# First layer of a hybrid decoder step: in 8 of 24 units a chunk's second part moves directly ahead of the next chunk's first part

## The chip, the cores and the metric

The kernel runs on one core of one Trainium2 chip. The metric is the device time of one launch in microseconds; the time before is the median of three runs. Profiles come from one separate, profiled execution.

## The reference

One inference step of a two-layer decoder with model width 1024, for a prompt of 512 positions and 8 samples of 4 positions, which share the weights. The first layer is a Mamba-2 (SSD) mixer with 32 heads of 64 in 4 groups, state size 128; the second is a dilated sliding-window attention. The heart of the first layer, where the change lies, is the chunked scan (T = 128, four chunks for the prompt):

```python
a_cs = jnp.cumsum(A, axis=-1)
seg = jnp.exp(jnp.where(tri, a_cs[..., :, None] - a_cs[..., None, :], -jnp.inf))
cb = jnp.einsum("bctgn,bcsgn->bcgts", Cc, Bc)
m = jnp.einsum("bcgts,bgjcts->bcgjts", cb, seg)
y_diag = jnp.einsum("bcgjts,bcsgjp->bctgjp", m, X)
chunk_states = jnp.einsum("bctgn,bgjct,bctgjp->cbgjpn", Bc, decay_in, X)
...
y_off = jnp.einsum("bctgn,cbgjpn,bgjct->bctgjp", Cc, s_in, jnp.exp(a_cs))
```

In words: each chunk builds a decaying causal mask m, gives an output within the chunk from m, hands a state to the next chunk, and adds what the incoming state contributes. Ahead of it stand a norm, the input projection and a convolution of width 4 with SiLU; behind it a gate with z, a norm and the output projection. The samples do the same for their 4 positions from a given state.

## The kernel before

All large products (projections, attention) run on TensorE (PE) with weights split into a high and a low part: a weight tile is loaded by the SP queue (wraw, L196), copied to whi by ScalarE (ACT, L205), and the rest goes to wlo on VectorE (DVE, L206). One projection tile is 48 matmuls, 24 into the PSUM tile pa and 24 into pb. In the first layer these matmuls are *filler*: a generator (filler_a, L882) yields after each of them, and run(n) (L899) takes n.

Between stretches of filler stand 24 *units*, for each of 4 groups of heads: chunk 0, chunk 1, quad 0, chunk 2, chunk 3, quad 1. A chunk (ssm_chunk, L720) is 128 prompt positions; a quad (ssm_quad, L782) is four samples.

A chunk has two parts, divided by a yield.

- First part: the mask tile m is loaded by the SP queue (L728; a row of cumulated decays, spread over all partitions, 512 KB) and turned into a decay on ACT (L730 eight times, L732). TensorE makes cbp (a transpose and a product) and xp (four transposes of xs). ACT copies btok, DVE makes xdt, xdd (L746, L747), cbm (L748) and multiplies m by it (L749). For chunks 1 to 3 the tile ea is loaded (L754).
- Second part: TensorE makes csp from xdd and btok, yo from the old state (chunks 1 to 3) and yd from m and xdt. POOL (GpSimd) and DVE form the new state st (L761, L762; chunk 0: a copy on ACT, L769), DVE makes ea from yo (L767) and v from yd and ea (L778; chunk 0: a copy on ACT, L776).

A quad has three parts: loads of sample states s (L804) and small products; yds, yot and three updates up, each added to s on DVE (L862) and written back (L863, ACT's queue); and a fourth update.

Buffers: m has two, xdt and xdd share three, ea has one, s five, wraw three, whi and wlo two each. In PSUM the tag ss (all tiles of units) has five buffers and the tag pj (pa, pb) three.

The loop at L915 places the parts. For unit u: first part of u, pace // 2 filler matmuls, second part of u-1, the rest of the pace, third part of u-1. The pace per unit is 57, 62, 64 or 44, by group. A chunk's third call finds its generator at its end. skip_one (L698) puts a skip product (L703) and the gate (L711) on DVE and POOL; its four calls per unit stay where they are.

The order of each engine's instructions is fixed ahead of the run by the framework's scheduler: it follows program order as priority, and takes an instruction when, by its own estimate of times, the inputs and a buffer are ready. Matmuls and transposes are held in program order from L430 on (pin, L139). Each engine, and the SP queue, then works down its list and waits where an input or buffer is late.

The tiles named in the steps are: wraw, whi, wlo (weights), cb, co, xs (convolution, L343 to L645), m, cbm, xdt, xdd, csp, yo, yd, st, ea, v (chunks), s, up (quads).

Of the kernel before, what the change touches and what calls it, by code (L numbers as in the profile page):

```python
# [127 lines left out]
def tile_yoco_step(  # L128
# [569 lines left out]
    def skip_one():  # L698
        if not skips:
            return  # L700
        g, i = skips.pop(0)
        vi = v_t[g][:, i, :]
        nc.vector.scalar_tensor_tensor(vi, xs_t[g][:, i, :], dsk[:, 4 * g + i:4 * g + i + 1], vi, op0=ALU.mult, op1=ALU.add)  # L703
        v_done.add((g, i))
        if i < z_done.get(g, 0):
            gate_mul_a(g, i)
# [192 lines left out]
    def run(n):  # L899
        for _ in range(n):  # L900
            if next(fill, 0) == 0:
                return

    units = [(f, (g, i)) for g in range(4) for f, i in
             ((ssm_chunk, 0), (ssm_chunk, 1), (ssm_quad, 0), (ssm_chunk, 2), (ssm_chunk, 3), (ssm_quad, 1))]
# [8 lines left out]
    live = []  # L914
    for u in range(len(units) + 1):  # L915
        pace = PACE[min(u, len(units) - 1) // 6]
        if u < len(units):
            live.append(units[u][0](*units[u][1]))
            next(live[u])
        skip_one()  # L920
        run(pace // 2)
        if u:
            next(live[u - 1], 0)
            skip_one()
            run(pace - pace // 2)
            next(live[u - 1], 0)
            if u == len(units):
                run(10000)
            if u % 6 == 0:
                skips += [(u // 6 - 1, i) for i in range(4)]  # L930
            skip_one()
        else:
            run(pace - pace // 2)
# [702 lines left out]
    def run(n):  # L1636
        m = min(n, ahead[0]) if n > OCN else 0
        ahead[0] -= m
        for _ in range(n - m):
            if next(fill, 0) == 0:  # L1640
                return

    units = [(f, (h, i)) for h in range(ATH - 1) for f, i in
             ((attend, 0), (sample, 0), (attend, 1), (attend, 2), (sample, 1), (attend, 3))]
# [6 lines left out]
    live = []  # L1651
# [113 lines left out]
```

## Time and profile before

| | us |
|---|---|
| median of three runs | 927.66 |
| lowest and highest | 925.65, 928.69 |
| profiled execution, its own time | 932.11 |
| its span | 930.2 |

The profile's span is the stretch from the first to the last recorded instruction; 1.9 us of the execution lie around it. Rows of a timeline give the start in us from the span's start, the duration, the engine, the line, the operation, and what was written and read; a bracket at the end gives the idle time just before it and what ended it. Several like instructions in a row are merged ("x3"). Rows of waits give who waited, on which line, for whom: total us, times, longest. Rows of windows give, for a stretch, its length and the busy time (and count) of PE, PEld, DVE, ACT and POOL, then the granted TensorE clock, the busy share of the DMA engines and GB/s. PEld is TensorE's loading of weights, which overlaps its matmuls.

### The profile page before, as it was taken

The page shows a single profiled execution, that of the slowest core. Times are in us where ns is not written, and L with a number is a line of the kernel's source. Part 1 is how long each engine was busy: PE and PEld are TensorE (multiplying, and loading weights), DVE is VectorE, ACT ScalarE, POOL GpSimd, SP SyncE. Part 2 cuts the span into 40 slices and gives each one's busy share as a digit, 9 for nine tenths or more (in the row PEclk, how much of TensorE's full clock was granted, in tenths as well). Part 3 has the DMA queues.
Part 4 walks back from the last instruction along what each step waited for, and adds up shares of the span by engine and source line. Part 5 has one row for each costly group of instructions (what it writes and reads, how often), then busy time and mean ns, then how long its engine had stood idle before and what let it go on. Part 6 is the DMA issues. An engine that isn't in the chain of part 4 may idle for free.

```text
span 930.2 us, 21888 instructions
## 1 busy us (share of the span) xinstructions
PE 908.9 (98%) x8671; PEld 847.9 (91%) x8671; DVE 687.5 (74%) x1435; ACT 489.9 (53%) x1140; POOL 163.0 (18%) x212
## 2 busy tenths in 40 slices
PE   8999999999999999999999999999999999999997
PEld 7989888888989889999999999999899999989997
DVE  6998899989799899644489335876677766778732
ACT  6678655655566655422255213555455555557642
POOL 2031344433514642111101001000000000000021
PEclk9999999999999999999999999999999999999999
DMA  8224365355364442536277556757768868774511
GB/s 295 93 74 155 104 206 166 121 170 170 134 201 161 149 165 101 156 108 228 90 256 227 183 184 196 265 182 264 252 203 262 280 204 267 270 256 155 194 49 49
DMA packets 80573, 168.48 MB, mean 181 GB/s; under 512 B 19990, under 2 KB 37736, under 8 KB 79960
## 3 DMA queue, kind: packets, MB, share of 16 engines
q1 hardware_dynamic: 73784, 154.60, 50.5%
q10 hardware_dynamic: 5616, 9.75, 2.8%
q0 software_dynamic: 1072, 2.74, 1.1%
q8 instruction: 68, 1.11, 0.5%
q14 instruction: 33, 0.27, 0.1%
HBM read 141.14 MB, written 25.93 MB: 180 GB/s over the span
## 4 chain that ended last, share of the span: by engine, by line
PE 82%; DVE 9%; DMA 4%; ACT 2%; issue 2%; POOL 0%; SPq 0%; POOLq 0%; DVEq 0%; ACTq 0%
PE pa L146 33%; PE pb L146 28%; PE sp L146 3%; PE pv L146 2%; PE so L146 2%; PE s L146 2%; DVE wlo L206 2%; DMA kc<-ck 1%; PE yd L146 1%; DMA m<-aed 1%; DVE co L641 1%; PE csp L146 1%; PE w L149 1%; PE ptp L149 1%; PE xp L149 1%
## 5 line engine op out<-in xcount | busy, mean ns | idle before, releaser
L205 ACT ACTIVATE whi<-wraw 128x1024 fp32r<-128x1024 f32 x69 | 72.8, 1056 | 97.0 <-PE pb L146 57.2
L206 DVE TENSOR_TENSOR wlo<-wraw,whi 128x1024 fp32r<-128x1024 f32 x69 | 89.6, 1298 | 45.1 <-ACT whi L205 44.7
L146 PE MATMUL pa<-bq,whi 128*128 128x272 f32 x512 | 103.1, 296 | 0.0
L146 PE MATMUL pb<-nl,whi 128*128 128x288 f32 x280 | 84.0, 300 | 0.0
L146 PE MATMUL pb<-nh,wlo 128*128 128x288 f32 x280 | 83.5, 298 | 0.0
L146 PE MATMUL pb<-nh,whi 128*128 128x288 f32 x280 | 83.4, 298 | 0.0
L146 PEld LDWEIGHTS pa<-bq,whi 128*128 128x128 f32 x512 | 81.2, 189 | 0.9
L146 PE MATMUL pa<-nh,whi 128*128 128x256 f32 x280 | 81.1, 290 | 0.5 <-DVE uz L681 0.5
L146 PE MATMUL pa<-nl,whi 128*128 128x256 f32 x280 | 80.7, 288 | 0.0
L146 PE MATMUL pa<-nh,wlo 128*128 128x256 f32 x280 | 80.1, 286 | 0.0
L146 PE MATMUL pb<-bq,whi 128*128 128x272 f32 x384 | 77.2, 296 | 1.3 <-DVE kv L1230 1.1
L146 PE MATMUL pa<-bq,wlo 128*128 128x272 f32 x256 | 74.2, 290 | 0.0
L641 DVE SCALAR_TENSOR_TENSOR co<-cb,cvp,co 128x568 f32<-128x568 f32 x72 | 64.0, 892 | 1.5 <-ACT co L639 0.9
L146 PEld LDWEIGHTS pb<-bq,whi 128*128 128x128 f32 x384 | 60.8, 189 | 2.6 <-DVE kv L1230 1.3
L1289 ACT ACTIVATE whi<-wraw 128x512 fp32r<-128x512 f32 x64 | 40.1, 627 | 35.2 <-PE pb L146 16.8
L146 PEld LDWEIGHTS pb<-nl,whi 128*128 128x128 f32 x280 | 53.0, 189 | 4.4 <-issue 4.4
L146 PEld LDWEIGHTS pa<-nh,whi 128*128 128x128 f32 x280 | 53.8, 192 | 2.6 <-issue 1.9
L146 PE MATMUL pb<-bq,wlo 128*128 128x272 f32 x192 | 55.5, 289 | 0.0
L146 PEld LDWEIGHTS pa<-nl,whi 128*128 128x128 f32 x280 | 53.8, 192 | 1.4 <-issue 1.4
L146 PEld LDWEIGHTS pb<-nh,wlo 128*128 128x128 f32 x280 | 53.1, 190 | 2.2 <-issue 2.2
L146 PEld LDWEIGHTS pa<-nh,wlo 128*128 128x128 f32 x280 | 53.8, 192 | 0.9 <-issue 0.9
L146 PEld LDWEIGHTS pb<-nh,whi 128*128 128x128 f32 x280 | 53.0, 189 | 0.8 <-issue 0.8
(408 smaller groups left out, 2788.0 us busy)
## 6 DMA issues: line engine op xcount, KB each, us to landing
wraw<-w_in SPq DMA_DIRECT2D x40, 512.0 KB
kc<-ck SPq DMA_DIRECT2D x32, 640.0 KB
vc<-cv SPq DMA_DIRECT2D x32, 640.0 KB
wraw<-wb SPq DMA_DIRECT2D x32, 512.0 KB
s<-s SPq DMA_DIRECT2D x32, 256.0 KB
m<-aed SPq DMA_DIRECT2D x16, 512.0 KB
ssmS<-s ACTq DMA_DIRECT2D x32, 256.0 KB
wraw<-w_out SPq DMA_DIRECT2D x16, 512.0 KB
```

What stands on the lines that cost most here:

```text
L146: pin(nc.tensor.matmul(*a, **k))
L149: pin(nc.tensor.transpose(*a))
L205: a = nc.scalar.activation(hi, raw, AF.Copy)
L206: b = lo_eng.tensor_tensor(lo, raw, f32(hi), op=ALU.subtract)
L641: nc.vector.scalar_tensor_tensor(o, cb[:, k:k + n], cvp[:, ti, k:k + 1], o, op0=ALU.mult, op1=ALU.add)
L1289: nc.scalar.activation(hi, src[p][j], AF.Copy)
```

## The change

Where unit u-1 and unit u are both chunks (chunks 0 and 1, chunks 2 and 3 of each group: 8 units), the second part of u-1 is called directly ahead of the first part of u, and no longer between the two stretches of filler behind it. Everything else, the filler's amounts included, stays.

```diff
     for u in range(len(units) + 1):
         pace = PACE[min(u, len(units) - 1) // 6]
+
+        joined = 0 < u < len(units) and units[u - 1][0] is units[u][0] is ssm_chunk
+        if joined:
+            next(live[u - 1], 0)
         if u < len(units):
             live.append(units[u][0](*units[u][1]))
             next(live[u])
         skip_one()
         run(pace // 2)
         if u:
-            next(live[u - 1], 0)
+            if not joined:
+                next(live[u - 1], 0)
             skip_one()
             run(pace - pace // 2)
-            next(live[u - 1], 0)
+            if not joined:
+                next(live[u - 1], 0)
             if u == len(units):
                 run(10000)
```

## The prediction

> **What bounds the kernel now.** I read the page's engine rows first, then the list of waits for the first layer, then the timeline around each wait of TensorE. The page says that TensorE sets the time.
>
> ```profile
> span 930.2 us, 21888 instructions
> PE 908.9 (98%) x8671; PEld 847.9 (91%) x8671; DVE 687.5 (74%) x1435; ACT 489.9 (53%) x1140; POOL 163.0 (18%) x212
> ```
>
> TensorE is busy for 908.9 of 930.2 us. The change neither adds nor removes a matmul, so it can win or lose only through TensorE's waits, its clock, and the switches between kinds of matmul. In the first layer's stretch of the trace the list of waits has these of TensorE, in total, count and longest:
>
> ```profile
> PE xp L149 <- DVE xs L644: 2.1, 1, 2.1
> PE up L146 <- DVE cbm L748: 1.4, 1, 1.4
> PE yd L146 <- ACT yos L825: 1.2, 1, 1.2
> ```
>
> They cost more than they show. Around the first two, the table by windows (busy time of the engines, then the granted clock) reads:
>
> ```profile
> 187.00:198.00 11.00, 11.00 (x92) 10.23 (x92) 11.00 (x18) 5.97 (x19) 0.40 (x1) 1.00 0.71 232
> 215.60:219.10 3.50, 3.50 (x18) 3.50 (x18) 3.50 (x6) 3.09 (x9) 0.00 (x0) 0.51 0.37 90
> 260.00:263.40 3.40, 3.40 (x17) 3.40 (x16) 3.38 (x8) 2.03 (x4) 0.00 (x0) 0.51 0.27 106
> ```
>
> Behind the wait of 2.1 us the granted clock is 0.51 for 3.50 us, which loses 3.50 x 0.49 = 1.7 us; behind the wait of 1.4 us it is 0.51 for 3.40 us, again 1.7 us. So the first costs 2.1 + 1.7 = 3.8 us (call it stall B, at 214 us), the second 1.4 + 1.7 = 3.1 us (stall C, at 258 us). The third cost its 1.2 us alone.
>
> The Trainium skill ("TensorE: Matmul & The Clock Gate", Part 1: The HAM clock gate) states that the clock halves after at least one idle window of about 3.4 us. The trace agrees on the halving and on how long it lasts (0.51 for 3.4 and 3.5 us), but not on the trigger: waits of 2.1 and 1.4 us were enough. By the page's trigger stall B would be worth its wait alone, and with the 0.4 us for switches below the forecast would be 927.66 - 0.4 - 2.1 = 925.2.
>
> Where do the stalls come from? For stall B, the timelines of the SP queue, ACT, DVE and TensorE, in order of time:
>
> ```profile
> 189.12 6.29 SPq L804 DMA_DIRECT2D s<-s  x3
> 195.46 0.42 SPq L196 DMA_DIRECT2D wraw<-w_in  x1
> 195.97 0.38 SPq L728 DMA_DIRECT2D m<-aed  x1
> ...
> 203.81 0.99 ACT L730 ACTIVATE m<-m,tok 128x128 f32<-128x128 f32 x3 [3.10 <-DMA m<-aed]
> 206.34 1.05 ACT L205 ACTIVATE whi<-wraw 128x1024 fp32r<-128x1024 f32 x1
> ...
> 207.42 1.23 DVE L206 TENSOR_TENSOR wlo<-wraw,whi 128x1024 fp32r<-128x1024 f32 x1 [3.11 <-ACT whi L205]
> 213.57 0.68 DVE L644 SCALAR_TENSOR_TENSOR xs<-cb,co 128x512 f32<-128x512 f32 x1
> 214.30 0.33 PE L149 MATMUL xp<-ident,xs 128*128 128x128 f32 x1 [2.14 <-DVE xs L644]
> ```
>
> This is one chain. The mask tile m of group 2's chunk 0 is loaded late (195.97); ACT, which works strictly down its list here, stands 3.10 us for it; the weight split behind it comes late, DVE stands 3.11 us for that, its convolution ends late, and TensorE stands 2.14 us. m has two buffers, so this load waits for the second part of the chunk two before, group 1's chunk 2, which reads its m in the yd matmuls.
>
> **What the change moves.** In 8 places the second part of a chunk comes ahead of the following chunk's first part instead of half a unit's filler behind it. One place now (unit 10, TensorE's timeline without filler), and the filler behind it:
>
> ```profile
> 186.52 0.50 PE L146 MATMUL up<-xr,btr 32*128 32x512 f32 x1
> 186.95 0.33 PE L149 MATMUL cbp<-ident,BT 128*128 128x128 f32 x1
> 187.34 0.60 PE L149 MATMUL xp<-ident,xs 128*128 128x128 f32 x4
> 191.79 1.02 PE L146 MATMUL csp<-xdd,btok 128*128 128x512 f32 x2
> 193.63 1.09 PE L146 MATMUL yd<-m,xdt 128*64 128x128 f32 x16
> ...
> 194.66 0.39 PE L146 MATMUL pa<-nh,whi 128*128 128x256 f32 x1
> 194.88 0.27 PE L146 MATMUL pa<-nl,whi 128*128 128x256 f32 x1
> 195.00 0.28 PE L146 MATMUL pa<-nh,wlo 128*128 128x256 f32 x1
> ```
>
> *Inputs of the moved part.* The second part needs xdt, xdd, btok and the masked m (DVE L749). The tightest of the 8 is the first:
>
> ```profile
> 81.43 1.22 DVE L749 TENSOR_TENSOR m<-m,cbm 128x1024 f32<-128x1024 f32 x1
> 84.56 0.28 PE L149 MATMUL cbp<-ident,BT 128*128 128x128 f32 x1
> 84.89 0.60 PE L149 MATMUL xp<-ident,xs 128*128 128x128 f32 x4
> ```
>
> m is ready at 82.65, the moved block begins at 84.56, and its yd comes behind csp (about 0.95 us). So 1.9 us remain to its start and 2.9 us to yd; elsewhere there is more. No new wait by before's order. The following chunk's cbp and xp come 2 to 3 us later, but its own second part is still a unit and a half away.
>
> *Switches.* The first filler matmul behind a block takes 194.88 - 194.66 = 0.22 us to the next one, the second 0.12. That 0.10 us is paid behind every block, and 8 blocks fewer save at most 0.8 us. What the new seam from yd to cbp costs the trace does not show. The nearest row is up to cbp: cbp comes 0.43 us behind up, and the spacing behind it (187.34 - 186.95 = 0.39) is 0.06 wider than that of a block that follows filler (84.89 - 84.56 = 0.33). A seam of that kind gives back about half of the 0.10; two of them make the saving nothing. So between 0 and 0.8 us is saved, a loss of some tenths is not excluded, and I take 0.4.
>
> *Buffers freed earlier.* This is the main term. In the place shown the second part starts at 186.95 instead of 191.79, 4.84 us earlier, so yd ends at 193.63 + 1.09 - 4.84 = 189.9. Then m, ea and a buffer of xdt/xdd are free 4.84 us earlier. The SP queue's waits show that this matters:
>
> ```profile
> SPq L728 <- PE yd L146: 10.6, 5, 4.6
> ACT m L730 <- DMA m<-aed: 12.9, 8, 3.6
> ```
>
> Five m loads were issued the moment yd ended, and ACT stood 12.9 us for eight of them. The load of 195.97 may go out between 189.9 (6.1 us earlier) and 195.46 (right behind the three state loads s, 0.5 us earlier); ACT needs 3.1. The queue's order is fixed ahead by the framework's own clock, and only what frees up earlier there moves. The third s of this run waits for an update written back behind 186.52, so it is itself free only some microseconds later than the new end of yd, and I expect m ahead of it. Then the 3.10 on ACT goes, the 3.11 on DVE goes with it, xs ends about 3 us earlier, near 211.2, and xp, which began to wait at 214.30 - 2.14 = 212.16, finds it ready. What is late next there is DVE's list itself, which is full; its margin is 1 us. Stall B goes: 3.8 us.
>
> Stall C hangs on two such waits of ACT:
>
> ```profile
> 237.80 0.42 SPq L728 DMA_DIRECT2D m<-aed  x1
> 243.04 0.69 ACT L730 ACTIVATE m<-m,tok 128x128 f32<-128x128 f32 x2 [3.64 <-DMA m<-aed]
> 250.54 0.38 SPq L728 DMA_DIRECT2D m<-aed  x1
> 254.88 0.99 ACT L730 ACTIVATE m<-m,tok 128x128 f32<-128x128 f32 x3 [1.45 <-DMA m<-aed]
> ```
>
> The first load (chunk 2's) waits for a moved part and comes earlier; the second (chunk 3's) waits for chunk 1's second part, which stays, and is issued behind a weight load. It gains only if the first 3.64 pass through to the weights. I leave stall C in the forecast.
>
> *Sum.* From the profiled execution's 932.11 us: -0.4 - 3.8 = -4.2, hence 927.9. The three timed runs have a median of 927.66, 4.45 us below the profiled one, so a stall may be smaller in them; I take the same difference off the median: **923.5 us**.
>
> **The rivals.**
>
> *Both stalls go* (0.20): the 3.64 pass through, the weight split and the load at 250.54 come 3 us earlier, cbm too. -0.4 - 3.8 - 3.1 = -7.3: 920.4. For it: both loads begin from the same kind of wait. Against: the second one's buffer is not freed earlier.
>
> *The SP order keeps m behind the s loads, or the timed runs lack the stalls* (0.32): only the switches remain, -0.4: 927.3. For it: the 4.45 us by which the timed runs are shorter. That the change does not do what it says I hold at nearly nothing: matmuls and transposes are held in program order (L139 to L149), so TensorE's order moves as written.
>
> *Slower: the PSUM buffers run out* (0.15). Tag ss has five buffers. In the four places with chunks 2 and 3, up, csp, yo, yd, cbp and xp follow one another, six tiles, so xp waits until DVE has read up (s, L862) or csp. How soon that is:
>
> ```profile
> 188.58 0.68 DVE L862 TENSOR_TENSOR s<-up,s 128x512 f32<-128x512 f32 x1
> 225.80 0.49 PE L146 MATMUL up<-xr,btr 32*128 32x512 f32 x1
> 232.79 0.68 DVE L862 TENSOR_TENSOR s<-up,s 128x512 f32<-128x512 f32 x1
> ```
>
> xp would come about 0.43 + 2.87 (csp to the end of yd, 191.79 to 194.66) + 0.4 = 3.7 us behind up. At 186.52 the read ends 188.58 + 0.68 - 186.52 = 2.7 us behind up: 1.0 us to spare. At 225.80, where only five tiles meet, it ended 7.7 us behind. If DVE is as late as that in one of the four places, xp waits 7.7 - 3.7 = 4.0 us and the clock takes 1.7 more: 5.7 - 0.4 = +5.3: 933.0. It decides from the point where the read of up ends later than 3.7 us behind it.
>
> *Slower: the clock drops in the joined blocks* (0.03). The joined block is up to 0.43 + 2.87 + 0.7 = 4.0 us of short matmuls. At 1.7 us a drop, 8 drops would be +13.6: 941. Against: the existing block of 2.87 us lies in 187 to 198 us, where the clock is 1.00. The Trainium skill (same page, "A second HAM failure mode: psum-queue depth-cycling") says that frequent short idles between groups make the clock swing; this trace shows no drop without a wait of at least 1.4 us.
>
> **How the numbers follow.** About 0.3% (2.8 us) is what a measurement of this kernel can tell from no change. The forecast has 0.30; at -0.45% a little of it falls within 0.3%. Faster: 0.20 + 0.27 = 0.47. Within: 0.03 + 0.32 = 0.35. Slower: 0.15 + 0.03 = 0.18. Below, the range takes in both stalls and the full 0.8 of the switches, 927.66 - 7.7 = 920.0; above, it reaches into the PSUM case, 931.0, and leaves out a full wait there and the clock drops.
>
> **What would show it.** Right: the m load of group 2's chunk 0 issued ahead of the weight load before it, and about 3 to 5 us earlier against the matmuls around it; ACT's wait for m well under 12.9 us; no wait of xp for xs in group 2; a clock of 1.00 there. In TensorE's timeline, csp directly behind up or filler and cbp directly behind yd, eight times. Wrong: ACT's waits for m unchanged, or xp waiting for s L862 or st L762 with a clock of 0.5 behind it. A saving of more than 2 us without a change in these waits would mean that the switches cost more than 0.10 us.

## The result and the profile after

The changed kernel takes 940.31 us (median of 6 runs, 936.66 to 941.75), the kernel before 927.94 us beside it: a ratio of 1.0129, 95% interval 1.0108 to 1.0151. It is 1.3% slower, 12.4 us, and lies above the range of 920.0 to 931.0 us. The profiled execution of the changed kernel took 940.48 us, as its timed runs do; the one of before, 932.11 us, lay 4.2 us above its median, so the two traces differ by 8.1 us of span only.

The page's first lines of the changed kernel:

```profile
span 938.3 us, 21895 instructions
PE 912.3 (97%) x8671; PEld 850.8 (91%) x8671; DVE 687.2 (73%) x1435; ACT 488.3 (52%) x1140; POOL 167.6 (18%) x212
```

TensorE's matmuls are the same (x8671), so the 8.1 us are waiting and clock. The list of waits of the changed kernel in the first layer (total, times, longest):

```profile
PE xp L149 <- DVE xs L644: 6.7, 2, 3.4
...
PE pa L146 <- DVE uz L681: 1.3, 2, 1.2
PE pa L146 <- DVE wlo L206: 1.3, 2, 1.1
PE yd L146 <- ACT yos L825: 1.1, 1, 1.1
PE xp L149 <- DVE xdd L832: 1.0, 2, 0.8
...
ACT m L730 <- DMA m<-aed: 30.4, 10, 8.5
```

The wait of xp for the convolution (xs), 2.1 us in one place before, is now 6.7 us in two; the wait of up for cbm is gone. ACT's wait for the mask, which was to shrink from 12.9 us, has grown to 30.4; its three longest parts, 4.7, 8.5 and 7.4 us, are all for masks of a chunk 0. The table by windows of the changed kernel, from the start of the chain to the stretches behind the two long waits (granted clock third from the end):

```profile
191.00:202.00 11.00, 11.00 (x92) 9.82 (x89) 6.50 (x11) 1.20 (x5) 2.30 (x5) 1.00 0.76 229
214.90:218.20 3.30, 0.02 (x1) 0.00 (x0) 3.30 (x7) 1.93 (x8) 0.00 (x0) 0.69 0.81 309
218.27:222.97 4.70, 4.70 (x22) 4.70 (x23) 4.70 (x9) 4.17 (x10) 0.22 (x1) 0.50 0.31 74
295.44:301.47 6.03, 6.03 (x39) 5.80 (x39) 5.00 (x9) 4.34 (x11) 2.30 (x2) 0.50 0.42 119
```

Behind the long waits the clock is 0.50 for 4.70 and 6.03 us, which loses half of it, 5.4 us in all. The five waits sum to 11.4 us, so the changed trace holds 16.8 us of such loss in this part. The same sum for before is 8.8 us: the three waits shown (2.1 + 1.4 + 1.2), two short ones (0.7) and twice 1.7 of clock. The difference, 8.0 us, is the 8.1 us of span but for 0.1. (Outside this part the changed trace has 1.7 us more of clock loss, at 48.9 us, and 1.5 us less of waits, which nearly cancel.) The first row shows where the loss begins: in 191 to 202 us ACT works 1.20 of 11 us, where it worked 5.97 in 187 to 198 us before.

The timelines of the SP queue, ACT, DVE and TensorE of the changed kernel, for the same mask as in the prediction:

```profile
190.24 3.38 SPq L804 DMA_DIRECT2D s<-s  x2
193.68 0.42 SPq L728 DMA_DIRECT2D m<-aed  x1
...
201.55 0.40 ACT L730 ACTIVATE m<-m,tok 128x128 f32<-128x128 f32 x1 [8.49 <-DMA m<-aed]
201.86 1.04 ACT L205 ACTIVATE whi<-wraw 128x1024 fp32r<-128x1024 f32 x1
...
202.94 1.23 DVE L206 TENSOR_TENSOR wlo<-wraw,whi 128x1024 fp32r<-128x1024 f32 x1 [5.44 <-ACT whi L205]
...
217.53 0.68 DVE L644 SCALAR_TENSOR_TENSOR xs<-cb,co 128x512 f32<-128x512 f32 x1
218.27 0.48 PE L149 MATMUL xp<-ident,xs 128*128 128x128 f32 x1 [3.35 <-DVE xs L644]
```

It is the chain of before with larger numbers, and the weight split that stands behind the Relu is now an earlier one: mask load, ACT, weight split, DVE, convolution, xp. Before, ACT had made that weight's high part ahead of the mask:

```profile
191.50 1.06 ACT L205 ACTIVATE whi<-wraw 128x1024 fp32r<-128x1024 f32 x1 [1.25 <-PE pb L146]
```

But the load itself is earlier. Against the update up ahead of it (before at 186.52, now at 187.79, below) it went out after 9.45 us before and after 5.89 us now, and ACT got it 17.3 us before and 13.8 us now behind up. The load took as long as before, 7.8 us from issue to use (203.81 - 195.97) and now 7.9 (201.55 - 193.68). What moved further than the load is its reader. ACT came to the first Relu and began to wait 14.2 us behind up before (203.81 - 3.10 - 186.52) and 5.3 us behind it now (201.55 - 8.49 - 187.79): 8.9 us earlier, where the load is usable 3.5 us earlier. The 5.4 us between the two are the growth of the wait from 3.10 to 8.49. The weight copy went the other way, from 5.0 us behind up (191.50 - 186.52) to 14.1 (201.86 - 187.79).

The cause is the order of ACT's list. Its instructions from the btok copy of the previous chunk on, in the order of the compiled programs (Rn: n Relu steps of this mask, L730; exp: L732; whi: a weight's high part; th: the convolution's Tanh, L643; others left out):

```
before:  btok  whi  th  th  R3  yos  R4  whi  R1  exp
changed: btok  R1  whi  th  R1  R3  R3  exp  yos
```

The first Relu, which stood behind the weight copy and two Tanh steps, now stands ahead of all three. The scheduler works with its own estimate of when the buffer comes free and the load lands; that the earlier release is what moved the Relu is tested below.

### The profile page after: what moved, and what is told of

It is laid out like the page before. It is cut to its first block, busy times and chain, and to the rows that moved or that the text cites. A ratio compares the mean times of both kernels' runs of the same rounds, so it can differ in the third digit from the quotient of the medians.

```text
span 938.3 us, 21895 instructions
## 1 busy us (share of the span) xinstructions
PE 912.3 (97%) x8671; PEld 850.8 (91%) x8671; DVE 687.2 (73%) x1435; ACT 488.3 (52%) x1140; POOL 167.6 (18%) x212
## 4 chain that ended last, share of the span: by engine, by line
PE 80%; DVE 9%; DMA 5%; ACT 4%; issue 2%; POOL 0%; SPq 0%; POOLq 0%; DVEq 0%; ACTq 0%
PE pa L146 33%; PE pb L146 27%; PE sp L146 3%; PE pv L146 2%; PE so L146 2%; DVE co L641 2%; PE s L146 2%; DMA m<-aed 2%; PE yd L146 1%; DMA kc<-ck 1%; PE csp L146 1%; PE w L149 1%; PE ptp L149 1%; PE xp L149 1%; DVE v L703 1%
## 5 line engine op out<-in xcount | busy, mean ns | idle before, releaser
L1295 ACT ACTIVATE whi<-wraw 128x512 fp32r<-128x512 f32 x64 | 40.1, 626 | 35.5 <-PE pb L146 16.8
L730 ACT ACTIVATE m<-m,tok 128x128 f32<-128x128 f32 x128 | 42.4, 395 | 30.4 <-DMA m<-aed 30.4
```

Source lines behind the costliest of these rows:

```text
L730: nc.scalar.activation(m_t[:, h, :], m_t[:, h, :], AF.Relu, scale=-1.0, bias=tok[:, c, 0, 8 * g + h:8 * g + h + 1])
L1295: nc.scalar.activation(hi, src[p][j], AF.Copy)
```

## The experiments

**Theory A**: the mask buffer that is freed earlier lets the scheduler put the mask's decay ops too high in ACT's list; ACT stands for the load, and the weights, the convolution and TensorE follow. **Theory B**: the joined order itself costs, by DVE work bunched behind the block or by PSUM buffers. Times of before in the two series have medians of 927.46 us (25 runs) and 928.18 us (29 runs).

**Only chunks 0 and 1 joined.** The load freed earlier is then chunk 2's.

```diff
-joined = 0 < u < len(units) and units[u - 1][0] is units[u][0] is ssm_chunk
+joined = 0 < u < len(units) and units[u - 1][0] is units[u][0] is ssm_chunk and u % 6 == 1
```

> Only chunk 0's second part is moved ahead of chunk 1 (4 of the 8 places). Theory A (the earlier freed mask buffer lets the scheduler place the next mask's decay ops higher in ACT's list than its load really lands; ACT stands, the weight split and the convolution come late, TensorE stalls): the load that moves is chunk 2's, whose waits in the changed kernel were 2.6 us or none and caused no stall of TensorE, so 925 to 931. Theory B (the joined order itself costs: DVE work bunched behind the block, PSUM buffers): half of the 12.4 us, about 934.

Measured: 929.30 us, ratio 1.0012 (0.9991 to 1.0033). Waits of this kernel:

```profile
PE xp L149 <- DVE xs L644: 0.9, 1, 0.9
PE up L146 <- DVE xdd L747: 0.8, 1, 0.8
...
ACT m L730 <- DMA m<-aed: 15.6, 9, 3.8
```

Half of the joined places cost nothing that can be told, and ACT's wait stays near the 12.9 us of before.

**Only chunks 2 and 3 joined.** The same line with `u % 6 == 4`; the load freed earlier is that of the next group's chunk 0.

> Only chunk 2's second part is moved ahead of chunk 3 (the other 4 places). Theory A: the load that moves is that of the next group's chunk 0, for which ACT stood 4.7, 8.5 and 7.4 us in the changed kernel; nearly the whole loss, 936 to 941, with TensorE waiting for xs at two group borders. Theory B: half, about 934.

Measured: 941.39 us, ratio 1.0157 (1.0107 to 1.0207), from four runs of which one took 948.43; it lies 0.4 us above what theory A gave. Waits of this kernel:

```profile
PE xp L149 <- DVE xs L644: 6.6, 2, 3.3
PE yd L146 <- ACT yos L825: 3.9, 3, 2.4
...
ACT m L730 <- DMA m<-aed: 29.6, 11, 9.4
```

The whole loss is here, with the same two waits of xp and about the same wait of ACT. (yd waits for ACT's yos copy 2.8 us longer here than in the changed kernel.) Theory B, which shared the loss between the halves, does not fit; but chunks 2 and 3 also make the longer blocks, so their order was still to be told from their masks.

**The changed kernel with the mask ops of chunks 0 and 2 queued behind the quad ahead.** TensorE's order and the freeing of the buffer stay; only ACT's list is held (nothing waits for the yos copy to end, it just goes first).

```diff
-        for h in range(8):
-            nc.scalar.activation(m_t[:, h, :], m_t[:, h, :], AF.Relu, ...)
-        nc.scalar.activation(m_t, m_t, AF.Exp, scale=-1.0)
+        with tc.issue_after(yos_ins[-1]) if c % 2 == 0 and yos_ins else nullcontext():
+            for h in range(8):
+                nc.scalar.activation(m_t[:, h, :], m_t[:, h, :], AF.Relu, ...)
+            nc.scalar.activation(m_t, m_t, AF.Exp, scale=-1.0)
...
-        nc.scalar.copy(yos, yo)
+        yos_ins.append(nc.scalar.copy(yos, yo).ins)
```

> The changed kernel, but the decay ops (Relu and Exp of m) of chunks 0 and 2 are queued in ACT's list behind the yos copy of the quad before; TensorE's order and the moment at which the mask buffer is freed stay as in the changed kernel. Theory A: ACT's waits of 7 to 8 us for m go, TensorE's waits for xs go, 920 to 930. Theory B: stays at 937 or above.

Measured: 927.03 us, ratio 0.9981 (0.9958 to 1.0004). All of the 12.4 us is gone. Waits of this kernel, then the timelines of the SP queue and ACT at the mask followed above:

```profile
PE pa L146 <- DVE wlo L206: 1.5, 2, 1.4
PE pa L146 <- DVE uz L681: 1.3, 2, 1.2
ACT m L731 <- DMA m<-aed: 11.1, 7, 4.0
```

```profile
192.09 0.42 SPq L728 DMA_DIRECT2D m<-aed  x1
194.32 1.06 ACT L205 ACTIVATE whi<-wraw 128x1024 fp32r<-128x1024 f32 x1 [2.69 <-PE pb L146]
...
201.27 0.57 ACT L825 COPY yos<-yos 128x512 f32<-128x512 f32 x1
201.74 1.28 ACT L731 ACTIVATE m<-m,tok 128x128 f32<-128x128 f32 x4
```

The load goes out 5.7 us behind up (at 186.36), as early as in the changed kernel (5.9). The weight copy is back ahead of the mask, the Relu steps begin at 201.74 without a wait, 9.7 us behind the load's issue, and xp no longer waits for xs at all. TensorE's order and the early load are kept and the loss is gone, so theory A is shown and theory B falls.

**The changed kernel with the mask loads held to their old time.** The load waits for the filler matmul behind which the second part used to stand.

```diff
+            if joined: old_end[4 * (u // 6) + (0 if u % 6 == 1 else 2)] = last_mm[0]
...
-        dma(m_t, dap(aed, ...))
+        md = dma(m_t, dap(aed, ...)); hold_m(md, 4 * g + c - 2)   # a wait for old_end[...]
```

> The changed kernel, but the mask loads whose buffer is now freed earlier wait for the filler matmul behind which the second part used to stand, so they go out at about the old time; TensorE's order stays joined. Theory A: ACT's list falls back to about that of before, 924 to 931. Theory B: stays at 937 or above.

Measured: 931.40 us, ratio 1.0031 (1.0009 to 1.0053), 0.4 us above what theory A gave. Waits of this kernel, then ACT's timeline at the same mask:

```profile
PE pa L146 <- DVE wlo L206: 2.2, 2, 2.0
PE xp L149 <- DVE xs L644: 1.4, 2, 1.1
...
ACT m L730 <- DMA m<-aed: 11.0, 8, 2.9
```

```profile
196.26 1.06 ACT L205 ACTIVATE whi<-wraw 128x1024 fp32r<-128x1024 f32 x1 [2.69 <-PE pb L146]
...
201.30 0.99 ACT L730 ACTIVATE m<-m,tok 128x128 f32<-128x128 f32 x3 [1.40 <-DMA m<-aed]
```

The load goes out at 196.75, 8.4 us behind up (at 188.31), and with it the Relu falls back behind the weight copy: it is the release that moved ACT's list. With a later load the kernel is 8.9 us faster than with the early one. That is the plainest form of it: most of what the joined order loses, it loses through the early release. About 0.3% stays; here TensorE once waits 2.0 us for wlo (at 164.9) and then has 3.41 us at a clock of 0.50, a wait that I have not followed further.

**The kernel before with the rule of the third experiment.**

> The kernel before (nothing joined) with the same rule for ACT's list: the decay ops of chunks 0 and 2 behind the yos copy of the quad before. Beside the run of the changed kernel with that rule (927.0 us) it shows what the joined order is worth by itself once the mask work no longer stands too early. Theory A: the same time as that run within 3 us (924 to 930), since the joined blocks brought no wait of their own; TensorE's wait for xs at 214 us and that for cbm at 258 us shrink or go. Theory B: clearly below it, 922 or less.

Measured: 925.77 us, ratio 0.9971 (0.9955 to 0.9987), the lowest median of all. Waits of this kernel:

```profile
PE pa L146 <- DVE uz L681: 2.0, 2, 1.2
PE yd L146 <- ACT yos L825: 0.9, 1, 0.9
...
ACT m L731 <- DMA m<-aed: 10.3, 8, 2.7
```

The waits at 214 and 258 us of the old trace are gone here, too. Between this kernel and the changed one with the same rule (0.9971 and 0.9981, intervals that overlap) no gain of the joined order can be seen.

**The changed kernel with the rule for chunk 0 alone** (`c == 0` in the condition).

> The changed kernel with the rule for chunk 0's mask alone; chunk 2's decay ops stay where the scheduler puts them. Theory A, with the loss in the loads that the joins of chunks 2 and 3 free: 925 to 931, ACT's waits of 8.5 and 7.4 us gone and the short ones of chunk 2's masks left. If chunk 2's masks carry half of the loss: about 934.

Measured: 928.12 us, ratio 1.0004 (0.9988 to 1.0021), with this wait:

```profile
ACT m L731 <- DMA m<-aed: 13.6, 8, 3.9
```

So the masks of chunk 0 carry all of the loss that can be told.

**The changed kernel with the rule for all masks** (chunks 1 and 3 behind the btok copy of the chunk ahead).

> The changed kernel with the rule for all masks: chunks 0 and 2 behind the yos copy of the quad before, chunks 1 and 3 behind the btok copy of the chunk before. Theory A: ACT's waits for m fall below the 11 us that are left with the rule for chunks 0 and 2; 922 to 928, at best 0.5% below before. If the remaining waits are covered: 927 as before.

Measured: 926.42 us, ratio 0.9990 (0.9976 to 1.0004), with this wait:

```profile
ACT m L731 <- DMA m<-aed: 3.0, 4, 1.6
```

ACT's wait falls from 11.1 to 3.0 us and the time does not follow. So what was left of that wait costs nothing that can be told.

## Why the prediction was wrong

**The step that failed** is the one under *Buffers freed earlier*: "Then the 3.10 on ACT goes, the 3.11 on DVE goes with it, xs ends about 3 us earlier". The load did come earlier, by 3.6 us against the matmuls around it and ahead of the next weight load, inside the bounds given and by more than the 3.1 us that ACT was said to need. But the step set the new arrival of the load against the old place of its reader in ACT's list. I had written that the SP queue's order follows the scheduler's own clock; the same holds for ACT's list, and ACT reached the first Relu 8.9 us earlier. The 3.10 us became 8.49, the 3.11 on DVE 5.44 (for the weight split before that one), the 2.14 of xp 3.35 (and 0.79 ahead of it), and a second border, with 3.35 us at 295 us, joined them. The list of waits of before could not tell a late load from an early reader, and I read the eight waits of ACT for m as late loads. For stall B the runs do not say which it was. In the run of before with the rule the stall went and ACT's wait at this mask was 1.06 us, but ACT came to the Relu only 0.5 us later against up, and the load took 6.1 us where it had taken 7.8. The Trainium skill's page "TensorE: Matmul & The Clock Gate" (Part 1, the paragraph on engine queue depths) says that ACT is strictly first in, first out; the trace agrees, the weight copy at 201.86 stood 8.49 us behind one Relu.

**How late a load lands.** The mask needed 7.9 us here and 4.6 us in the run with the held loads (196.75 to 201.30). The page "DMA: Bandwidth & Descriptors" of the Trainium skill (Anatomy of one DMA) fits 2.0 us plus the bytes at 436 GB/s for loads on the GpSimd path, an estimate of 3.2 us for 512 KB. The changed kernel's trace has more than twice that, beside loads and writes of states.

**Stall C.** I left it in; it went (no wait of up for cbm in the changed trace). The load of chunk 3's mask went out 22.7 us behind up (253.02 - 230.33) where it had been 24.7 (250.54 - 225.80), which fits the chain of the first rival; no run takes that chain apart. Stall B, which was to go, grew.

**The switches.** Here are TensorE's rows of the joined block at unit 10, then DVE's read of up:

```profile
187.79 0.50 PE L146 MATMUL up<-xr,btr 32*128 32x512 f32 x1
188.21 1.12 PE L146 MATMUL csp<-xdd,btok 128*128 128x512 f32 x2
189.18 1.05 PE L146 MATMUL yo<-CT,st 128*128 128x128 f32 x8
190.16 1.09 PE L146 MATMUL yd<-m,xdt 128*64 128x128 f32 x16
191.19 0.33 PE L149 MATMUL cbp<-ident,BT 128*128 128x128 f32 x1
191.35 0.39 PE L146 MATMUL cbp<-CT,BT 128*128 128x128 f32 x2
191.57 0.60 PE L149 MATMUL xp<-ident,xs 128*128 128x128 f32 x4
```

```profile
189.71 0.69 DVE L862 TENSOR_TENSOR s<-up,s 128x512 f32<-128x512 f32 x1
```

From up to the next quad's cbp it takes 199.84 - 187.79 = 12.05 us, before 198.58 - 186.52 = 12.06. Taken like this, the eight places together are 0.16 us shorter, against the 0.4 taken. The switches are worth next to nothing.

**Inputs and rivals.** No input of a moved part was late, as said. The PSUM rival did not come: up is read 189.71 + 0.69 - 187.79 = 2.6 us behind its start, 3.8 us passed until xp, and xp did not wait in any joined block. The clock did not drop in a joined block. So the slower side had 0.18, but for two mechanisms that did not happen; the one that did was not among the rivals.

**What stays open.** In the profiled executions the difference is 8.1 us, in the timed ones 12.4. The profile of before holds stalls B and C, and its time lies near the top of the 925.08 to 933.13 us of 25 of its runs. The mean granted clock of every timed run is on record: of these 25 runs, the six at 0.999 or 1.000 took 925.08 to 926.61 us and the seven at 0.992 to 0.995 took 927.42 to 933.13, so the drops of the clock occur in some runs and not in others. The changed kernel's six runs have 0.989 to 0.993 (median 0.992, before 0.997); 0.5% of 930 us is an estimate of 4.7 of the 12.4 us. Which wait stood behind a drop in a timed run is not on record.

## What to carry to other kernels

Where a scheduler orders every engine's list ahead of time, freeing a buffer earlier moves not only the load but also its readers, and a reader that stands in a list before its load has landed holds up everything behind it. So ask of each load that comes earlier where its first reader now stands and which critical work is behind that reader; holding the reader behind an instruction near its use was worth 1.5% in the changed kernel and 0.3% in the kernel before. A wait for a load in a trace can mean a late load or an early reader, so look at the list on both sides of it before calling it either.

## What the runs showed of the hardware

In the traces of before and changed, the waits of TensorE of 1.4 and 2.1 us and the two of 3.35 us were followed by 3.4, 3.4, 4.70 and 6.03 us at a clock of about 0.50, so these four stalls cost 1.7 to 2.2 times what the list of waits shows. The length of the wait does not settle it. With only chunks 2 and 3 joined, a wait of 2.37 us (at 136.7) was followed by no drop, and the waits of 3.27 and 3.35 us by 3.41 us at 0.50 each. With only chunks 0 and 1 joined, a wait of 0.79 us behind 1.9 us of short matmuls (at 316.3) was followed by 3.41 us at 0.50. So the clock has to be read behind each wait, run by run; what decides it no run here shows. And the switch between kinds of matmul, 0.10 us behind a block as the rows of the filler show it, did not come back when eight blocks were joined to others: 0.02 us each.
